# Dilated attention's third head group: 64x64 class blocks in place of masked 128x128 tiles

## The chip, the core and the metric

One core of a Trainium2 chip runs the whole program, one transformer sub-layer for 1024 tokens in float32. The metric is the device time of one execution in microseconds. The program uses TensorE (PE, with its weight loads shown apart as PEld), VectorE (DVE), ScalarE (ACT), GpSimd (POOL), and SyncE (SP), which issues nearly all DMAs.

## The reference, cut to what matters

The block has three mixers beside each other. The change touches the first, a sliding-window attention in three head groups, of window and dilation (128, 1), (512, 4), (2048, 16), with eight heads of 64 each:

```python
def dilated_window_attention(q, k, v, window, dilation):
    half = window // (2 * dilation)                  # 64 in each group
    L = s // dilation                                # 1024, 256, 64
    # regroup positions into residue classes mod dilation, each of L positions
    ...
    valid = (|qpos - kpos| <= half) & (0 <= kpos < L)
    sc = where(valid, q @ k * dh ** -0.5, -1e30)
    m = max(sc); p = exp(sc - m); l = sum(p)
    return (p / l) @ v, m + log(l)

outs, lses = one of these per group
wts = softmax(stack(lses), axis=0)
oa = einsum('gbsh,gbshd->bshd', wts, stack(outs))
```

In the third group the dilation is 16, so there are 16 classes of 64 positions, and with a half window of 64 each position of a class sees all 64 positions of its own class and nothing else. A tile of 128 queries, ordered by class, holds two classes: of its 128 x 128 scores with the same 128 keys, only the two diagonal blocks of 64 x 64 count.

## The kernel before

The program is one long run of PE work in stages: norms and key/value projections, the axial attention, value and key projections of the dilated attention, the dilated attention itself, then the merge gates, the three output branches and the last projection. The dilated attention takes the stretch from 716 to 987 us.

Its work is cut into twelve *items*, one for each pair of heads `p_` (four) and group `g` (three), in the order of `seq` (L1721), the third group of a pair last. While an item runs, PE also computes the dense query projection of an item two further on (`dense`, L139: 48 matmuls of 128 x 128 by 128 x 512 in each of two halves, float32r). `weave` (L176) lays the two streams into one order: it gives every piece of an item a cost, and between two pieces it issues as many dense matmuls as that cost is of the item's total. The order of ACT, DVE, POOL and SP in this stretch is the order in which the program writes the instructions; nothing reorders them.

An item works on eight tiles `T` of 128 queries, for both heads of its pair. `plan` (L1571) lists its pieces:

- `values(x)` (L1408): DMAs on SP that bring one half of V from DRAM to `vfull` (shown as `avs`), and for groups one and two also to `vpart` (`avp`). For the third group there are two per half, L1414, one for each class of a tile, with 64 partitions and pieces of 128 floats (both heads).
- `scores(b)` (L1449): for four tiles, the query tile of each head (64 rows of the array, the head's own half) times the keys, into PSUM banks of pool `s1` (four). Two tiles share a pair of banks. The two heads of a tile write different banks. L1466 in the profile.
- `soft(T)` (L1469): for each head a DVE instruction that adds the mask and takes the minimum of a row (L1478; the queries carry a minus sign), then an exponential with its row sum on ACT (L1479). Results lie in `pra`, five buffers.
- `trans(T)` (L1482): the probabilities are transposed on PE, one 128 x 128 transpose for each head and block of keys (L1505 where a tile has no 64-key blocks, L1496 otherwise), into a bank of pool `t` (two), and ACT copies them to `app` (L1508), six buffers. It comes `LAG` = 3 tiles behind `soft`: `trans(T - 3)` is written ahead of `soft(T)`, the last three in the next item.
- `pv(b)` (L1511): for four tiles, V of a head (64 weight columns, so the head's own column half of the array) times the transposed probabilities, all into one bank of pool `t` (L1522); ACT copies it out (L1530). `pv(0)` comes at `T` = 7, `pv(1)` at `T` = 3 of the next item, each followed by the `scores` of a half.
- `stats` (L1532): minima and sums are transposed and sent to DRAM; with them `combine` (L1634) weighs the three groups of a pair, in pieces that fall into the next pair's first two items.

`window` (L40) gives the keys of a tile and where its mask lies. In the third group a tile has one block of keys, its own 128; the mask at columns 256 to 383 lets a query see its own class only. The sums then hold exact zeros for the other class.

Of the kernel before, what the change touches and what calls it, by code (L numbers as in the profile page):

```python
# [8 lines left out]
F32 = mybir.dt.float32  # L9
# [8 lines left out]
P = 128  # L18
# [20 lines left out]

def window(g, T):  # L40
    if g == 2:
        return T * 128, T * 128 + 128, 256
    L = S // DIL[g]
    c0 = (T * 128) // L * L
    lo = max(T * 128 - 64, c0)
    hi = min(T * 128 + 192, c0 + L)
    return lo, hi, lo - (T * 128 - 64)
# [3 lines left out]
def block(ctx: ExitStack, tc: tile.TileContext, x, xT, memT, cst, msk, bcst, tabA, gpost,  # L51
# [1251 lines left out]
    with tc.tile_pool(name="aa", bufs=1, reuse_waits="tile") as aa:  # L1303
# [95 lines left out]
        def item(p_, g):  # L1399
# [8 lines left out]
            def values(x):  # L1408

                v = vdr[g, p_]  # L1410
                if g == 2:
                    vv = v.rearrange("(u r) f -> u r f", r=16)
                    for z in range(2):
                        nc.sync.dma_start(vfull[z * 64:z * 64 + 64, 4 * x:4 * x + 4].rearrange("p b h d -> p b (h d)"),  # L1414
                                          vv[:, 8 * x + z:8 * x + 8:2])
                    return
                if g == 0:
                    b0, b1 = (0, 4) if x == 0 else (4, 7)
                    nc.sync.dma_start(vfull[:, b0:b1].rearrange("p b h d -> p b (h d)"),
                                      v[64 + 128 * b0:64 + 128 * b1].rearrange("(b q) f -> q b f", q=128))  # L1420
                else:
                    nc.sync.dma_start(vfull[:, 4 * x:4 * x + 2].rearrange("p b h d -> p b (h d)"),
                                      v.rearrange("(u r) f -> u r f", r=4)[64:192, 2 * x:2 * x + 2])
                for z in range(2):
                    zs, f = slice(z * 64, z * 64 + 64), slice(z * 64, z * 64 + 64)
                    if g == 0:
                        nc.sync.dma_start(vpart[zs, 4 * x, z], v[960 * x:960 * x + 64, f])
                    else:
                        for e in range(2):
                            nc.sync.dma_start(vpart[zs, 4 * x + e:4 * x + 4:2, z], v[768 * e:768 * e + 256].rearrange(  # L1430
                                "(q r) f -> q r f", r=4)[:, 2 * x:2 * x + 2, f])
# [17 lines left out]
            def scores(b):  # L1449
                if b == 0:  # L1450
                    d["ops"] = OPS.pop((p_, g))
                    d["sts"] = cb.tile([P, 2, 2, NT], F32, name="sts", bufs=2)
                qa, ka = d["ops"]["q"], d["ops"]["k"]
                for j in range(4):
                    T = 4 * b + j
                    lo, hi, _ = window(g, T)
                    n = hi - lo
                    if j % 2 == 0:
                        banks = [pss1(), pss1()]
                    raws[T] = [x[:, j % 2 * 256:j % 2 * 256 + n] for x in banks]  # L1460
                    for r in range(2):
                        for h in range(2):
                            if r < len(spans(T, h)):
                                k0, k1, c = spans(T, h)[r]
                                hs = slice(h * 64, h * 64 + 64)
                                PE.matmul(raws[T][h][:, c:c + k1 - k0], qa[hs, T * 128:T * 128 + 128], ka[hs, k0:k1],  # L1466
                                          start=True, stop=True)
# [14 lines left out]
            def trans(T):  # L1482
                lo, hi, mo = window(g, T)
                n = hi - lo
                pr = st[T]
                kb = blocks_of(T)
                tp = pst()
# [23 lines left out]
            def pv(b):  # L1511
                if b == 0:
                    d["og"] = OG[p_, g] = cb.tile([P, S], F32, name="og", bufs=4)
                og = d["og"]
                ov = pst().rearrange("p a b -> p (a b)")
                for j in range(4):
                    terms = st.pop(4 * b + j)
                    n = len(terms[0])
                    for i in range(n):
                        for h in range(2):  # L1520
                            (vt, x), z, pp = terms[h][i]
                            PE.matmul(ov[h * 64:h * 64 + 64, j * 128:j * 128 + 128], vt[:, x, z], pp,  # L1522
                                      start=i == 0, stop=i == n - 1)
                if g == 0:
                    dst, src = og[:, b * 512:b * 512 + 512], ov
                else:
                    r = DIL[g] // 2
                    dst = og.rearrange("p (u r) -> p r u", r=DIL[g])[:, b * r:b * r + r]
                    src = ov.rearrange("p (r u) -> p r u", r=r)
                A.activation(dst, src, AF.Copy)  # L1530
# [694 lines left out]
def layout(inp):  # L2225
# [42 lines left out]
    k = np.arange(256)[None]  # L2268
    m = np.zeros((P, 768), f)
    m[:, :256] = np.where(np.abs(p + 64 - k) <= 64, 0.0, 1e30)  # L2270
    m[:, 256:384] = np.where(p // 64 == k[:, :128] // 64, 0.0, 1e30)
    m[:, 384:576] = np.concatenate([m[:, 128:256], m[:, 64:128]], 1)
    m[:, 576:768] = np.concatenate([m[:, 128:192], m[:, 0:128]], 1)
    r['msk'] = m
# [55 lines left out]
```

## Time and profile before

| | |
|---|---|
| median of three runs | 1414.94 us (1414.56 to 1415.76) |
| profiled execution, from its first to its last instruction | 1412.1 us |
| dilated attention, 716 to 987 us | 271 us, PE busy 269.2 |
| scores of a half, third group (L1466, in the chain) | 1.09 us |
| product with V of a half, third group (L1522, in the chain) | 1.02 us |
| a pair of transposes between dense matmuls (L1505) | 0.22 us |

In the profile's rows, a group of instructions has its line, engine, operation, tiles written and read, shape (for PE the rows and columns of the array that are used, then the partitions and elements moved), count, busy time in us and mean ns of one. "<-" behind an idle time names what ended it. A busy PE is no proof of a full one, since matmuls overlap; the distance between starts tells more. Times in the rows of the timeline and the chain are us from the span's start, then the length.

### The profile page before, as it was taken

Reading aid. Unit: us, or ns where it says so; the run is one execution under the profiler, and the core shown is the slowest. Engines: PE = TensorE matmul, PEld = TensorE weight load, DVE = VectorE, ACT = ScalarE, POOL = GpSimd, SP = SyncE. Lnnn points to the kernel's source line nnn. Section 1 sums busy time; section 2 is a strip of 40 time slices with the busy share of each in tenths; the row PEclk is TensorE's granted clock in tenths of the full one; section 3 lists DMA queues with packets and bytes.
Section 4 is the critical chain, followed back from the end, with each engine's and each line's share of the span. In section 5 each row is a group of like instructions: output and inputs, shape, how many; then the busy total and the mean of one; then the engine's idle time right before and its main releaser. Section 6 shows DMA issues by size and latency. Waiting matters only on the chain.

```text
span 1412.1 us, 21576 instructions
## 1 busy us (share of the span) xinstructions
PE 1389.9 (98%) x7640; PEld 1126.2 (80%) x7640; DVE 1054.0 (75%) x1839; ACT 665.0 (47%) x1414; POOL 500.3 (35%) x390
## 2 busy tenths in 40 slices
PE   7999999999999999999999999999999999999997
PEld 7799986666666889888888878787888888888886
DVE  7768677767763688788875777765878788677977
ACT  6544365666555445222146666656443334222332
POOL 0416702666657000333153353520423331035303
PEclk9999999999999999999999999999999999999999
DMA  6356532322210787445643554555343543866255
GB/s 235 101 179 211 186 109 86 116 83 71 83 55 25 243 261 240 125 148 175 201 140 90 135 162 115 138 144 180 106 150 127 176 175 124 323 216 207 94 206 179
DMA packets 121852, 216.01 MB, mean 153 GB/s; under 512 B 25424, under 2 KB 58000, under 8 KB 121744
## 3 DMA queue, kind: packets, MB, share of 16 engines
q1 hardware_dynamic: 106096, 189.17, 42.0%
q10 hardware_dynamic: 15648, 25.47, 4.9%
q8 instruction: 60, 0.98, 0.3%
q14 instruction: 48, 0.39, 0.1%
HBM read 149.21 MB, written 65.37 MB: 152 GB/s over the span
## 4 chain that ended last, share of the span: by engine, by line
PE 88%; DVE 4%; ACT 3%; DMA 2%; POOL 2%; issue 1%; SPq 0%; DVEq 0%; ACTq 0%; POOLq 0%
PE s L125 23%; PE sc L125 9%; PE d L143 7%; PE d L147 6%; PE d L145 6%; PE s L1177 4%; PE s L2101 4%; PE ov L809 4%; PE s L1226 3%; PE tr L1522 3%; PE s L1466 3%; PE s L794 2%; PE s L793 2%; PE tr L775 2%; PE d L2101 2%; PE d L550 1%
## 5 line engine op out<-in xcount | busy, mean ns | idle before, releaser
L143 PE MATMUL d<-hh,wh 128*128 128x512 f32 x480 | 195.1, 406 | 2.4 <-DVE fth L228 2.4
L145 PE MATMUL d<-hl,wh 128*128 128x512 f32 x480 | 194.3, 405 | 0.0
L147 PE MATMUL d<-hh,wl 128*128 128x512 f32 x480 | 190.9, 398 | 0.0
L800 POOL TENSOR_TENSOR bl<-bl,bp 128x512 f32<-128x512 f32 x96 | 130.6, 1361 | 54.4 <-ACT bp L796 49.0
L105 ACT ACTIVATE wh<-wr 128x512 fp32r<-128x512 f32 (+1 forms) x93 | 72.5, 787 | 122.1 <-PE sc L125 75.3
L106 DVE TENSOR_TENSOR wl<-wr,wh 128x1024 fp32r<-128x1024 f32 (+1 forms) x67 | 85.3, 1285 | 50.2 <-ACT wh L105 50.2
L125 PE MATMUL sc<-hh,wh 128*128 128x512 f32 x384 | 118.5, 389 | 0.0
L143 PEld LDWEIGHTS d<-hh,wh 128*128 128x128 f32 x480 | 90.5, 188 | 27.8 <-issue 6.6
L147 PEld LDWEIGHTS d<-hh,wl 128*128 128x128 f32 x480 | 90.6, 189 | 21.0 <-issue 4.5
L1479 ACT ACTIVATE pra<-pra,sts 128x192 f32<-128x192 f32 (+2 forms) x192 | 84.3, 442 | 46.3 <-DVE sts L1478 45.8
L145 PEld LDWEIGHTS d<-hl,wh 128*128 128x128 f32 x480 | 90.6, 189 | 19.2 <-issue 4.5
L796 ACT ACTIVATE bp<-s 128x512 f32<-128x512 f32 x128 | 75.7, 595 | 43.3 <-PE s L794 42.3
L776 DVE TENSOR_REDUCE bn<-tr 128x1 f32<-128x512 f32 x128 | 84.9, 683 | 12.8 <-PE tr L775 11.7
L125 PEld LDWEIGHTS sc<-hh,wh 128*128 128x128 f32 x384 | 72.1, 188 | 14.9
L1330 DVE SCALAR_TENSOR_TENSOR t2a<-d,tab 32x512 f32<-32x512 f32 x96 | 65.9, 687 | 23.2 <-PE d L147 21.4
L2006 POOL TENSOR_TENSOR acc<-acc,th 128x1024 f32<-128x1024 f32 x15 | 41.4, 2757 | 109.1 <-DVE th L2005 109.1
L1789 POOL TENSOR_TENSOR sf<-wr 128x512 f32<-128x512 f32 x22 | 29.8, 1373 | 131.3 <-DVE ch L106 57.4
L125 PE MATMUL sc<-hl,wh 128*128 128x512 f32 x192 | 74.8, 389 | 0.0
L125 PE MATMUL s<-hh,ch 128*128 128x512 f32 x224 | 73.5, 390 | 0.0
L1334 POOL TENSOR_TENSOR aq<-t1a,t2a 128x512 f32<-128x512 f32 x24 | 44.6, 1861 | 72.0 <-DVE t1a L1333 72.0
L1819 ACT ACTIVATE rs<-rs,hbm 128x512 f32<-128x512 f32 x44 | 31.8, 722 | 76.5 <-DVE rs L1818 75.8
L1397 POOL TENSOR_TENSOR ak<-kraw,kswp 128x512 f32<-128x512 f32 x24 | 47.8, 2015 | 54.7 <-DMA std<-sr 21.2
(500 smaller groups left out, 3775.6 us busy)
## 6 DMA issues: line engine op xcount, KB each, us to landing
wr<-in_wu SPq DMA_DIRECT2D x64, 512.0 KB
th<-thd SPq DMA_DIRECT2D x24, 512.0 KB
thd<-rs ACTq DMA_DIRECT2D x44, 256.0 KB
kd<-vy ACTq DMA_DIRECT2D x32, 256.0 KB
g2d<-fth SPq DMA_DIRECT2D x24, 256.0 KB
wos<-os SPq DMA_DIRECT2D x12, 512.0 KB
kraw<-kd SPq DMA_DIRECT2D x12, 512.0 KB
kswp<-kd SPq DMA_DIRECT2D x48, 128.0 KB
```

The source lines that it names most:

```text
L105: A.activation(dst_h, src, AF.Copy)
L106: V.tensor_tensor(dst_l, src, dst_h.bitcast(F32), op=OP.subtract)
L125: PE.matmul(out_ps, a, b, start=i == 0, stop=i == n - 1)
L143: PE.matmul(dst, wh[:, k, :], hh[k][:, t], start=k == 0, stop=False)
L145: PE.matmul(dst, wh[:, k, :], hl[k][:, t], start=False, stop=False)
L147: PE.matmul(dst, wl[:, k, :], hh[k][:, t], start=False, stop=k == 7)
L776: fp["last"] = V.tensor_reduce(st[i]["n"][:, j, c:c + 1], s, axis=AX.X, op=OP.min)
L796: A.activation(pp, s, AF.Exp, scale=-1.0)
L800: G.tensor_tensor(lsum[i % 2], lsum[i % 2], pp, op=OP.add)
L1330: V.scalar_tensor_tensor(t2[i], p[j], -0.125, tab[1][j, t], op0=OP.mult, op1=OP.mult)
L1479: A.activation(src, src, AF.Exp, scale=-1.0, bias=bias, accum_out=sts[:, h, 1, T:T + 1])
L2101: PE.matmul(dst[:, e[0]:e[1]], a, b, start=k == 0 and q == 0, stop=k == 3 and q == 2)
```

## The change

For the third group (`g == 2`), and for nothing else:

- `scores`: each head's 128 x 128 product becomes two of 64 x 64, one for each class `z`. Query class `z` is the weight (64 rows, 64 columns) and writes the partitions `z` of the head's bank, 64 columns wide. Four matmuls for a tile in place of two.
- `window` gives 64 columns instead of 128, so `soft` works on 64 columns for a head, and the two heads lie beside each other in 128 columns of `pra`. The mask is not changed at the place where it is now read (columns 256 to 319, which are zero there since the line that wrote the class mask is gone).
- `trans`: one transpose of these 128 columns turns both heads of a tile at once. It is written only for odd `T`, for the tile and its even neighbour together, with one copy on ACT for both.
- `pv`: the transposed tile has head `h`'s keys on the partitions of that head, so V of head `h` and class `z` must lie on those partitions too. Four matmuls of 64 x 64 by 64 columns for a tile in place of two of 128 x 64 by 128.
- `values`: the DMAs bring one head each (64 partitions, 8 classes, pieces of 64 floats) in place of one class each.

```diff
 def window(g, T):
     if g == 2:
-        return T * 128, T * 128 + 128, 256
+        return T * 128, T * 128 + 64, 256
...
                 if g == 2:
                     vv = v.rearrange("(u r) f -> u r f", r=16)
-                    for z in range(2):
-                        nc.sync.dma_start(vfull[z * 64:z * 64 + 64, 4 * x:4 * x + 4].rearrange("p b h d -> p b (h d)"),
-                                          vv[:, 8 * x + z:8 * x + 8:2])
+                    for h in range(2):
+                        hs = slice(h * 64, h * 64 + 64)
+                        nc.sync.dma_start(vfull[hs, 4 * x:4 * x + 4].rearrange("p b z d -> p (b z) d"),
+                                          vv[:, 8 * x:8 * x + 8, hs])
                     return
...
                     raws[T] = [x[:, j % 2 * 256:j % 2 * 256 + n] for x in banks]
+                    if g == 2:
+                        for z in range(2):
+                            for h in range(2):
+                                hs, zs = [slice(i * 64, i * 64 + 64) for i in (h, z)]
+                                t = slice(T * 128 + z * 64, T * 128 + z * 64 + 64)
+                                PE.matmul(raws[T][h][zs], qa[hs, t], ka[hs, t], start=True, stop=True)
+                        continue
...
             def trans(T):
                 lo, hi, mo = window(g, T)
                 n = hi - lo
+                if g == 2:
+                    if T % 2:
+                        tp = pst()
+                        pp = aa.tile([P, 4, 128], F32, name="app", bufs=6)
+                        for z in range(2):
+                            PE.transpose(tp[:, z, :], st[T - 1 + z][:, 0:128], ident)
+                            st[T - 1 + z] = pp[:, z]
+                        A.activation(pp[:, :2], tp[:, :2], AF.Copy)
+                    return
...
                     terms = st.pop(4 * b + j)
+                    if g == 2:
+                        for z in range(2):
+                            for h in range(2):
+                                hs, zs = [slice(i * 64, i * 64 + 64) for i in (h, z)]
+                                PE.matmul(ov[hs, j * 128 + z * 64:j * 128 + z * 64 + 64], vfull[hs, 4 * b + j, z], terms[hs, zs],
+                                          start=True, stop=True)
+                        continue
...
     m[:, :256] = np.where(np.abs(p + 64 - k) <= 64, 0.0, 1e30)
-    m[:, 256:384] = np.where(p // 64 == k[:, :128] // 64, 0.0, 1e30)
```

## The prediction, made before the change was run

> **What bounds the kernel now.** I read the page's busy shares and chain first, then the sums of the stretch in which the dilated attention runs, then the chain through one of its third-group items.
>
> ```profile
> span 1412.1 us, 21576 instructions
> PE 1389.9 (98%) x7640; PEld 1126.2 (80%) x7640; DVE 1054.0 (75%) x1839; ACT 665.0 (47%) x1414; POOL 500.3 (35%) x390
> PE 88%; DVE 4%; ACT 3%; DMA 2%; POOL 2%; issue 1%; SPq 0%; DVEq 0%; ACTq 0%; POOLq 0%
> ...
> 716.00:987.00 271.00, 269.23 (x2068) 219.09 (x2066) 188.00 (x572) 174.92 (x560) 101.51 (x51) 1.00 0.49 136
> ```
>
> The last row has the columns PE, PEld, DVE, ACT, POOL busy, granted clock, DMA share, GB/s. PE idles 1.8 of 271 us there, at full clock, while DVE has 83 us free and ACT 96. A microsecond taken from PE's own stream is therefore nearly a microsecond off the end, and work taken from DVE or ACT counts only where PE waits for it. The chain through the first third-group item (start, length, what):
>
> ```profile
> 765.23 1.90 PE tr L1522 x32
> 767.12 1.09 PE s L1466 x16
> 768.22 0.37 PE tr L1505 x2
> ...
> 771.36 0.22 PE tr L1505 x2
> ...
> 774.59 1.02 PE tr L1522 x16
> 775.61 1.94 PE s L1466 x17
> ```
>
> L1466 is the scores of four tiles (half an item), L1505 the two transposes of a tile, L1522 the product with V for four tiles. Eight f32 matmuls show as 16 records, so a matmul is two passes. How passes share the array is read from the busy sums of one line over growing windows (length, PE busy, instructions begun):
>
> ```profile
> 774.52:774.67 0.15, 0.15 (x2) 1.00 0.00 0
> 774.52:774.78 0.26, 0.26 (x4) 1.00 0.00 0
> 774.52:774.89 0.37, 0.37 (x6) 1.00 0.00 0
> 774.52:775.34 0.82, 0.82 (x16) 1.00 0.00 0
> ...
> 767.05:767.26 0.21, 0.20 (x2) 1.00 0.00 0
> 767.05:767.37 0.32, 0.32 (x4) 1.00 0.04 6
> 767.05:767.48 0.43, 0.42 (x6) 1.00 0.03 5
> ```
>
> The first four are V's product, the rest the scores. Passes come in pairs, one pair per 0.11 us: both heads work at once, in two column halves of the array for V's product and in two row halves for the scores. So a half costs eight pair steps, 8 x 0.11 = 0.88 us, plus about 0.2 us to the next kind of work in the chain rows above (1.09 and 1.02).
>
> **The change, part by part.**
>
> *Transposes.* Per item eight pairs become four. A pair between dense matmuls costs PE 0.22 us (771.36). Four items: 16 x 0.22 = 3.5 us less. Nothing hides them now; they stand on the chain.
>
> *Scores.* Per tile two matmuls of 64 rows, 128 weight columns and 128 moved columns become four of 64, 64 and 64. Rows for the size of a pass (mean ns of one):
>
> ```profile
> L1466 PE MATMUL s<-ak,aq 64*128 64x128 f32 x208 | 25.0, 285 | 0.0
> L1466 PE MATMUL s<-ak,aq 64*128 64x64 f32 x80 | 13.2, 245 | 0.0
> L1466 PEld LDWEIGHTS s<-ak,aq 64*128 64x128 f32 x464 | 33.8, 187 | 5.1 <-issue 4.5
> L1522 PEld LDWEIGHTS tr<-app,avs 128*64 128x64 f32 x480 | 26.7, 137 | 9.5 <-ACT pra L1479 3.6 <-ACT wh L105 2.9 <-ACT app L1508 2.3
> ```
>
> 64 moved columns fewer shorten a matmul by 40 ns, 64 weight columns fewer shorten a load by 50 ns; both are about half of the 0.11 us step, so I take a 64 by 64 pass at 0.058 us. There are 32 passes in a half. If all four blocks of a tile (two heads, two classes) run together, that is eight steps: 8 x 0.058 = 0.46 us against 0.90, 0.44 less. If the two classes of a head take turns, it is 16 steps: 0.93, 0.03 more. A third bound is the rate at which PE takes instructions: a half will have 64 (loads and passes) instead of 32.
>
> ```profile
> 774.51 0.20 PEld L1522 LDWEIGHTS tr<-app,avs 128*64 128x64 f32 x4 [0.37 <-ACT wh L105]
> 774.52 0.33 PE L1522 MATMUL tr<-app,avs 128*64 128x128 f32 x2
> ```
>
> Four loads of 0.137 us lie within 0.20 us and two passes begin with them: six instructions in 0.06 us, 10 ns each, and so 64 in 0.64 us. I take 0.55, between 0.46 and 0.64: 0.35 less a half, 2.8 us in eight halves; bounds 3.5 less and 0.2 more.
>
> The Trainium skill states a floor that speaks against this: "TensorE: Matmul & The Clock Gate", Part 1, "Wait — 56ns, not 53.3ns?", has starts of matmuls never closer than about 25 ns, however small. By it a score half would be an estimated 32 x 25 = 0.80 us, and my sum would end at 1411.1. The two passes that begin together in the last row above speak against it for passes in different parts of the array.
>
> *Product with V.* Per tile two matmuls (128 rows, 64 weight columns, 128 moved) become four of 64, 64, 64, in diagonal quarters of the array: the heads can run side by side as now, the two classes of a head follow each other. 16 steps of 0.058 = 0.93 us for 0.87: 0.06 more a half, 0.45 us in all. Bounds: nothing more (16 x 0.055), or 0.87 more a half, 7.0 in all, if a step stays at the 0.109 us below which no f32 pair of passes lies in these windows. I take the low side because of the halved load and matmul rows.
>
> *DVE, ACT.* The masked minimum and the exponential of a tile and head shrink from 128 to 64 columns, and 16 of the 32 copies of 256 columns go:
>
> ```profile
> L1478 DVE CUSTOM_DVE_ANT_0 pra<-s,mask 128x192 f32<-128x192 f32 x80 | 24.8, 353 | 2.3 <-PE s L1466 1.8
> L1478 DVE CUSTOM_DVE_ANT_0 pra<-s,mask 128x128 f32<-128x128 f32 x64 | 15.7, 286 | 4.7 <-PE s L1466 4.5
> L1479 ACT ACTIVATE pra<-pra,sts 128x192 f32<-128x192 f32 x80 | 35.5, 446 | 25.7 <-DVE sts L1478 25.5
> L1479 ACT ACTIVATE pra<-pra,sts 128x128 f32<-128x128 f32 x64 | 25.0, 392 | 19.0 <-DVE sts L1478 19.0
> L1508 ACT ACTIVATE app<-tr 128x256 f32<-128x256 f32 x32 | 12.2, 381 | 6.6 <-PE tr L1505 6.4
> ```
>
> By the steps between sizes that is 67 ns of DVE and 54 of ACT for each of 64, 4.3 and 3.5 us, and 16 x 0.38 = 6.1 us of ACT. All of it lies beside PE and is worth nothing except at PE's idle times:
>
> ```profile
> 823.70 0.33 PE L1496 MATMUL tr<-cs,pra 128*128 128x128 f32 x1 [0.25 <-ACT app L1508]
> ...
> 885.98 0.33 PE L1496 MATMUL tr<-cs,pra 128*128 128x128 f32 x1 [0.22 <-ACT app L1508]
> ...
> 941.83 0.44 PE L1522 MATMUL tr<-app,avs 128*64 128x128 f32 x4 [0.80 <-ACT app L1508]
> ...
> 983.75 0.33 PE L1505 MATMUL tr<-cs,pra 128*128 128x128 f32 x1 [0.43 <-ACT og L1530]
> ...
> 818.03 2.53 DVE L1677 TENSOR_TENSOR og<-og,wgt 128x1024 f32<-128x1024 f32 x1
> 820.59 1.38 DVE L1330 SCALAR_TENSOR_TENSOR t2a<-d,tab 32x512 f32<-32x512 f32 x2
> 822.00 0.29 DVE L1478 CUSTOM_DVE_ANT_0 pra<-s,mask 128x128 f32<-128x128 f32 x1
> 822.39 0.40 ACT L1479 ACTIVATE pra<-pra,sts 128x128 f32<-128x128 f32 x1 [1.63 <-DVE sts L1478]
> 823.18 0.47 ACT L1508 ACTIVATE app<-tr 128x384 f32<-128x384 f32 x1
> ```
>
> At 823.70 and 885.98, just behind the first score half of an item, PE waits for a copy that ACT makes behind the item's first two exponentials, which wait for DVE, full since 818.03. That gate opens 0.067 + 2 x 0.054 = 0.17 us sooner, while PE comes 0.35 sooner: 0.17 of the scores' gain is lost at each, 0.35 us together. The 0.80 us at 941.83 lie in the second group's item and stay. At 983.75 PE waits with the last item's seventh pair of transposes, which no longer exists; the pair that comes later finds the copy done: 0.35 of the 0.43 us go (bounds 0 and 0.43).
>
> *Moved steps and waits.* An even tile's transpose is issued with its odd neighbour's, where that one's already stands, so the last pair ahead of V's product (771.36) keeps its place 3.2 us ahead of it, and its copy of 0.38 us its cover. The even tile's buffer lives one step longer: four of five are then in use. No new wait; PSUM banks for transposes are asked for half as often.
>
> *Loads of V.* Two DMAs a half as before, in pieces of 256 instead of 512 bytes. Queue rows of a stretch of 3.0 us with nearly only 512-byte packets, one of 2.7 us with 256-byte ones, and SP's issue:
>
> ```profile
> q1 hardware_dynamic: 544, 0.26, 30.5%
> ...
> q1 hardware_dynamic: 474, 0.11, 18.4%
> ...
> 769.29 1.28 SPq L1414 DMA_DIRECT2D avs<-vdr  x2
> ```
>
> A packet takes 0.305 x 16 x 3.0 / 544 = 27 ns, or 0.184 x 16 x 2.7 / 474 = 17 ns. A half load goes from 512 x 27 / 16 = 0.86 us of the engines to 1024 x 17 / 16 = 1.09. It is issued at 769.29 for a product near 784, a cover of over 10 us; what is behind it on SP (weights, raw keys) is used a unit later. Nothing, or 0.2 us at each of eight loads if that cover were gone.
>
> **Sum.** -3.5 (transposes) -2.8 (scores) +0.45 (V) +0.35 (gates) -0.35 (end) = -5.85 us on a span of 1412.1. The median of the runs, 1414.94, is 2.8 above that span, which I carry over: 1409.1 us.
>
> **Rivals.** *The two classes of a head take turns in the scores.* For it: no row shows all four quarters at work. Against it: the windows show column halves together and row halves together. Scores +0.2, V +0.45, no gate loss but the two gates 0.17 sooner (-0.35), end -0.35, transposes -3.5: -3.55, 1411.4 us. Chance 0.20.
>
> *The two heads take turns in the product with V.* They now use different row halves but still write one bank; the scores, which do use row halves, write two banks, so no row tests it. Then a half is 32 steps, 1.86 us, 0.93 more than in my sum, 7.4 in eight: +1.6, 1416.5 us, slower than before. It decides from four fifths of the passes on (5.85 of 7.4). Against it: V's product shows pairs in one bank today, though over all rows. The Trainium skill ("TensorEngine Tiling (Array Packing)", "Gotcha 1: PSUM Pressure") states that row tiles cannot access one bank at the same time; it has no word on row tiles that also differ in columns, and no row here shows it. Chance 0.12.
>
> *PE is fed too slowly.* In the 0.82 us window V's product takes 16 passes and as many loads, 26 ns each; were that its limit, a half of 64 would last 1.66 us, scores and V together 12.4 us more, and with -3.5 and -0.7 the end is +8.2, 1423.1 us. It decides from 18 ns on. Against it: the 10 ns above. Chance 0.09.
>
> *DVE and ACT gate more.* If half of the gain goes into waits of PE: 1412.0 us. For it: DVE full behind the score halves of two items; against: 83 us free. Chance 0.09.
>
> **How the numbers follow.** The forecast has 0.50, with its own range from 1407.0 (score half 0.46, V unchanged, all of the four idle times gone but the second group's) to 1410.8 (score half 0.75, idle times nearly as now). From 1407.0 to 1413.0 lie nearly all of it, the first rival and the last: 0.78. A measurement of this kernel tells about 0.2%, 2.8 us, from no change: faster (below 1412.1) is the forecast, the first rival and half of the last, 0.73; within, the rest of it and most of the heads' taking turns, 0.15; slower 0.12.
>
> **What will show it.** Score half in the chain: 32 passes in about 0.75 us instead of 16 in 1.09; windows with four passes per 0.058 us (right), two (classes take turns). V's half: 32 passes in about 1.08; near 2 us means heads taking turns. Of L1505's 160 transposes 64 go and 32 come at a new line. DVE's smallest form near 0.22 us. PE's idle times of 716 to 987 stay at 1.5 to 2.2 us; over 4 would mean that DVE and ACT gate. If both halves grow in step with their instruction count, the feed was the limit. A stage that ends 6 us sooner but an end that does not follow would refute that PE's stream sets the end.

## The result and the profile after

| | before | after |
|---|---|---|
| median of five runs each | 1414.94 us (1413.20 to 1415.76) | 1409.91 us (1409.67 to 1411.43) |
| ratio, 95% interval | | 0.9962 [0.9949, 0.9974] |
| profiled execution, span | 1412.1 | 1408.1 |
| first third-group scores to first matmul of the gates ("the stage" below) | 230.34 | 225.03 |
| PE idle from 716 to 987 us | 1.77 | 2.86 |

The change is 5.0 us faster by the medians; 1409.1 us was predicted. The page of the changed kernel, in the same order as before (span, busy times, shares of the chain):

```profile
span 1408.1 us, 22008 instructions
PE 1384.0 (98%) x7864; PEld 1120.3 (80%) x7864; DVE 1051.2 (75%) x1839; ACT 655.7 (47%) x1398; POOL 501.9 (36%) x390
PE 86%; DVE 4%; ACT 4%; DMA 2%; POOL 2%; issue 2%; SPq 1%; DVEq 0%; ACTq 0%; POOLq 0%
```

The attention stretch in the sums of windows:

```profile
716.00:987.00 271.00, 268.14 (x2315) 218.90 (x2314) 188.43 (x575) 169.33 (x551) 106.25 (x54) 1.00 0.50 137
```

PE still bounds, at full clock, but its idle time in the stretch has grown from 271 - 269.23 = 1.77 to 2.86 us. To see what the stage itself won, take the distance between two rows of the chain: the start of the first third-group score half and of the first gate matmul (L125). Before:

```profile
756.82 1.09 PE s L1466 x16
...
987.16 12.96 PE s L125 x56
```

After, with the rows of an item between them:

```profile
757.20 0.62 PE s L1467 x32
...
766.79 0.62 PE s L1467 x32
...
770.32 0.23 PE tr L1498 x2
...
783.73 1.08 PE tr L1539 x32
...
982.23 17.91 PE s L125 x78
```

987.16 - 756.82 = 230.34 against 982.23 - 757.20 = 225.03: 5.31 us less in the stage. The span shows only 4.0, since the start lies 0.38 later and the tail behind 982.23 is 0.93 longer (425.87 for 424.94), in a part that the change does not touch; two later runs (the pair without key adds, below) have equal tails of 425.30, so that is not counted against the change. The median is 2.8 us above the span before (1414.94 - 1412.1) and 1.8 after; in every run of the kernel of before beside the experiments below a run's time is 1.7 to 1.8 above its own span. So the profiled execution of before was about 1 us quicker than the median, which fits the span's 4.0 beside the median's 5.0.

The score half went from 1.09 to 0.62 us, the product with V from 1.02 to 1.08. The sums of windows that grow from the start of one score half show why (length, PE busy, matmuls begun, clock):

```profile
766.72:766.76 0.04, 0.04 (x4) 1.00 0.07 10
766.72:766.82 0.10, 0.10 (x4) 1.00 0.04 4
766.72:766.88 0.16, 0.16 (x8) 1.00 0.40 105
...
766.72:766.99 0.27, 0.27 (x16) 1.00 0.24 62
```

Four passes begin together and four more every 0.055 to 0.06 us: all four quarters of the array work at once. The same for the product with V:

```profile
783.66:783.70 0.04, 0.04 (x2) 1.00 0.15 13
...
783.66:783.82 0.16, 0.16 (x4) 1.00 0.04 3
783.66:783.88 0.22, 0.22 (x6) 1.00 0.03 2
```

Two passes per 0.06 us: the heads run side by side in one bank, the two classes of a head in turn. The groups by line and shape:

```profile
L1486 DVE CUSTOM_DVE_ANT_0 pra<-s,mask 128x64 f32<-128x64 f32 x64 | 11.4, 219 | 3.8 <-PE s L1467 3.6
...
L1498 PE MATMUL tr<-cs,pra 128*128 128x128 f32 x32 | 6.3, 277 | 0.0
...
L1467 PE MATMUL s<-ak,aq 64*64 64x64 f32 x256 | 6.1, 225 | 0.1
```

32 transposes are left at the new line and the minimum fell from 286 to 219 ns, as said. What did not come out as said are the waits. PE's timeline:

```profile
823.64 0.33 PE L1513 MATMUL tr<-cs,pra 128*128 128x128 f32 x1 [0.95 <-ACT app L1525]
...
884.58 0.44 PE L1513 MATMUL tr<-cs,pra 128*128 128x128 f32 x2 [0.76 <-ACT app L1525]
```

These were 0.25 and 0.22. The waits of PE's weight loads, summed by what released them (sum, times, longest):

```profile
PEld s L1474 <- DVE sts L1486: 1.1, 3, 0.5
```

This one is new: at three *joints*, where an item's product with V is followed by the next item's first scores, these wait for banks that DVE frees with the third group's last minima. They do not show as idle time of PE, but in the distances between starts: from the first of these score matmuls to the next dense one it is 2.47, 2.13 and 2.31 us, and was 1.94 before. The third-group score half at 817.43 is late in the same way, 1.20 us to the next dense matmul instead of 0.62. The wait at 983.75 is gone. What DVE and POOL do ahead of 823.64, after:

```profile
815.09 0.69 DVE L106 TENSOR_TENSOR wl<-wr,wh 128x512 fp32r<-128x512 f32 x1 [1.40 <-ACT wh L105]
815.99 1.65 DVE L106 TENSOR_TENSOR wl<-wr,wh 128x512 fp32r<-128x512 f32 x1 [0.20 <-ACT wh L105]
...
818.11 2.56 DVE L1701 TENSOR_TENSOR og<-og,wgt 128x1024 f32<-128x1024 f32 x1
...
815.82 2.95 POOL L1397 TENSOR_TENSOR ak<-kraw,kswp 128x512 f32<-128x512 f32 x2 [4.93 <-DMA std<-sr]
...
824.99 1.29 POOL L1334 TENSOR_TENSOR aq<-t1a,t2a 128x512 f32<-128x512 f32 x1 [0.83 <-DVE t1a L1333]
```

and before:

```profile
816.87 0.69 DVE L106 TENSOR_TENSOR wl<-wr,wh 128x512 fp32r<-128x512 f32 x1 [0.20 <-ACT wh L105]
...
817.15 4.57 POOL L1397 TENSOR_TENSOR ak<-kraw,kswp 128x512 f32<-128x512 f32 x2 [5.37 <-DMA std<-sr]
```

L106 on DVE splits a weight tile for the dense projection, L1397 on POOL adds the two parts of the rotated keys. Before, DVE began first, its split took 0.69 us and POOL's two adds, which met the weighing at 818.03 as well, took 4.57. After, POOL began 0.17 us ahead, its two adds took 2.95 and DVE's split 1.65. The end of the split at 817.64 is what the last minima, the weighing at 818.11 and the third group's first minima queue behind. PE's stream had come 0.9 us sooner by then (a dense matmul at 787.90 of before begins at 787.03), while the weighing begins 0.08 later. Ahead of each of the three joints a pair of splits meets two of POOL's adds too: the pairs took 3.21, 2.87 and 3.05 us after (at 772.17, 834.21 and 895.15), 2.57, 2.51 and 2.53 before, and the joint behind the longest pair waits longest (0.52, 0.19 and 0.36).

The other place is different. DVE and POOL ahead of 884.58, after:

```profile
877.69 0.69 DVE L106 TENSOR_TENSOR wl<-wr,wh 128x512 fp32r<-128x512 f32 x1 [0.20 <-ACT wh L105]
...
878.85 2.76 DVE L1701 TENSOR_TENSOR og<-og,wgt 128x1024 f32<-128x1024 f32 x1
...
878.45 4.31 POOL L1397 TENSOR_TENSOR ak<-kraw,kswp 128x512 f32<-128x512 f32 x2 [5.85 <-DMA std<-sr]
```

Here the split is done before POOL begins and takes its 0.69 us. What lies beside the adds is the weighing: 2.76 us, where it took 2.53 before (at 880.31) and takes 2.0 in the runs without these adds, below. PE's score half is 0.47 shorter, the weighing 0.23 longer, and the way from its end to the start of ACT's copy 0.17 shorter (2.62 us before, 2.45 after): 0.47 + 0.23 - 0.17 = 0.53, and the wait grew by 0.54.

The Trainium skill ("SBUF — State Buffer", "Who interferes with whom") states that a DVE instruction with two SBUF inputs contends with a GpSimd instruction that reads SBUF, and it calls the ports that the two engines share an exclusive lock: the one that issues first has them for the whole instruction and the other is blocked (said there of DVE's two-port modes). The rows of this instruction agree with that to within 0.2 us: a split of 0.69 that starts beside an add of 1.29 us (the last row of POOL after, an add of the same shape by itself) would end at 815.82 + 1.29 + 0.69 = 817.80 if it stood through the whole add, and ended at 817.64. The weighing of 2.0 us, standing through the first add at the other place, would end at 878.45 + 1.29 + 2.0 = 881.74, and ended at 881.61.

### The profile page after: what moved, and what is told of

Read it like the earlier page. It is cut to its first block, busy times and chain, and to the rows that moved or that the text cites. A ratio compares the mean times of both kernels' runs of the same rounds, so it can differ in the third digit from the quotient of the medians.

```text
span 1408.1 us, 22008 instructions
## 1 busy us (share of the span) xinstructions
PE 1384.0 (98%) x7864; PEld 1120.3 (80%) x7864; DVE 1051.2 (75%) x1839; ACT 655.7 (47%) x1398; POOL 501.9 (36%) x390
## 3 DMA queue, kind: packets, MB, share of 16 engines
q8 instruction: 62, 1.02, 0.3%
## 4 chain that ended last, share of the span: by engine, by line
PE 86%; DVE 4%; ACT 4%; DMA 2%; POOL 2%; issue 2%; SPq 1%; DVEq 0%; ACTq 0%; POOLq 0%
PE s L125 24%; PE sc L125 9%; PE d L143 6%; PE d L147 6%; PE d L145 6%; PE s L1177 4%; PE s L2125 4%; PE ov L809 3%; PE s L1226 3%; PE s L794 2%; PE s L793 2%; PE tr L775 2%; PE d L2125 2%; PE s L1474 2%; PE tr L1546 1%
## 5 line engine op out<-in xcount | busy, mean ns | idle before, releaser
L106 DVE TENSOR_TENSOR wl<-wr,wh 128x1024 fp32r<-128x1024 f32 (+1 forms) x67 | 85.6, 1289 | 52.1 <-ACT wh L105 52.0
L125 PE MATMUL sc<-hh,wh 128*128 128x512 f32 x384 | 118.7, 390 | 0.0
L1487 ACT ACTIVATE pra<-pra,sts 128x192 f32<-128x192 f32 (+2 forms) x192 | 80.9, 423 | 54.3 <-DVE sts L1486 54.1
L125 PEld LDWEIGHTS sc<-hh,wh 128*128 128x128 f32 x384 | 72.0, 188 | 15.7 <-DVE wh L106 0.4
L125 PE MATMUL sc<-hl,wh 128*128 128x512 f32 x192 | 74.7, 389 | 0.0
L125 PE MATMUL s<-hh,ch 128*128 128x512 f32 x224 | 73.7, 390 | 0.0
L1397 POOL TENSOR_TENSOR ak<-kraw,kswp 128x512 f32<-128x512 f32 x24 | 45.9, 1939 | 51.7 <-DMA std<-sr 20.0
```

The costliest lines, as they stand in the source:

```text
L106: V.tensor_tensor(dst_l, src, dst_h.bitcast(F32), op=OP.subtract)
L125: PE.matmul(out_ps, a, b, start=i == 0, stop=i == n - 1)
L1487: A.activation(src, src, AF.Exp, scale=-1.0, bias=bias, accum_out=sts[:, h, 1, T:T + 1])
```

## The experiments

All stage lengths are read from the chain as above, PE idle time and the splits' mean from the windows and groups of 716 to 987 us. Ratios are to the kernel of before, run beside each set; its median was 1415.90 us beside e1, e2, e4 and e5, 1415.22 beside e3, e10, e8 and b8, and 1415.05 beside the rest, so runs of different sets are better compared by ratio than by median. The changed kernel was not run again in these sets. A difference from it carries two intervals, together about 2 us, and where it is smaller the reading rests on the traces, one execution each.

| run | median us | ratio, 95% interval | stage us | PE idle us | split L106, mean ns |
|---|---|---|---|---|---|
| before | 1414.94 | | 230.34 | 1.77 | 877 |
| after | 1409.91 | 0.9962 [0.9949, 0.9974] | 225.03 | 2.86 | 964 |
| e1_scores_only | 1412.52 | 0.9979 [0.9970, 0.9988] | 228.26 | 3.03 | 933 |
| e2_full_scores | 1413.33 | 0.9983 [0.9974, 0.9992] | 229.50 | 3.36 | 1005 |
| e4_weigh_earlier | 1411.94 | 0.9973 [0.9962, 0.9985] | 227.95 | 4.53 | 969 |
| e5_joints_later | 1411.87 | 0.9979 [0.9970, 0.9988] | 229.50 | 6.07 | 1033 |
| e3_own_transposes | 1411.82 | 0.9976 [0.9966, 0.9986] | 226.33 | 3.67 | 948 |
| e10_twice_transposed | 1410.85 | 0.9974 [0.9965, 0.9983] | 226.27 | 2.03 | 883 |
| e8_weigh_on_pool | 1413.44 | 0.9985 [0.9976, 0.9994] | 229.96 | 5.72 | 1147 |
| b8_before_weigh_on_pool | 1417.63 | 1.0019 [1.0010, 1.0028] | 234.00 | 3.74 | 1017 |
| e11_no_key_add | 1406.71 | 0.9941 [0.9927, 0.9954] | 222.01 | 1.18 | 777 |
| b11_before_no_key_add | 1413.73 | 0.9990 [0.9981, 0.9999] | 229.29 | 1.22 | 760 |
| e12_key_add_t7 | 1416.46 | 1.0013 [1.0004, 1.0022] | 231.37 | 6.54 | 1378 |
| e13_key_add_t6 | 1417.68 | 1.0021 [1.0012, 1.0030] | 231.87 | 7.22 | 1350 |

### The parts of the change

**The scores alone.** The kernel of before with the 64 x 64 score blocks and 64-column minima; transposes and product with V keep their number and shape.

```diff
+                    if g == 2:
+                        for z in range(2):
+                            for h in range(2):
...
+                                PE.matmul(raws[T][h][zs], qa[hs, t], ka[hs, t], start=True, stop=True)
+                        continue
...
-                            PE.transpose(tp[:, k, :], pr[:, h * n + c:h * n + c + 128], ident)
+                            PE.transpose(tp[:, k, :], pr[:, h * n * (g < 2) + c:h * n * (g < 2) + c + 128], ident)
```

> The kernel before with only the scores in 64x64 blocks and the softmax on 64 columns; two transposes a tile and V's product of 128 columns stay as before (they read the same 128 columns twice, so the third group's result is left out). Theory (PE's stream sets the end, but DVE and ACT hold PE at the places behind the first score half of an item): PE's score halves shrink by 0.47 us each, 3.8 us in eight, but 1.5 to 2 us come back as waits of PE, so 2 us less than before. Rival (all of PE's saving reaches the end): 3.8 us less.

Measured: 0.9979, 3.0 us faster by the ratio, and 2.08 less in the stage. Each score half is 0.62 us in the chain, 0.47 less, which makes 3.8 in eight; the waits rose at the same places as in the changed kernel, in PE's timeline to 0.96 at the first:

```profile
824.72 0.55 PE L1503 MATMUL tr<-cs,pra 128*128 128x128 f32 x3 [0.96 <-ACT app L1515]
```

So about 1.7 of the 3.8 us that PE saves on scores are waited away in this execution, as the theory said. The time does not decide: its interval, 1.7 to 4.2 us, holds the theory's 2 and the rival's 3.8.

**All but the scores.** The changed kernel with scores of 128 x 128 again.

```diff
-                        for z in range(2):
-                            for h in range(2):
-                                hs, zs = [slice(i * 64, i * 64 + 64) for i in (h, z)]
-                                t = slice(T * 128 + z * 64, T * 128 + z * 64 + 64)
-                                PE.matmul(raws[T][h][zs], qa[hs, t], ka[hs, t], start=True, stop=True)
+                        for h in range(2):
+                            hs = slice(h * 64, h * 64 + 64)
+                            t = slice(T * 128, T * 128 + 128)
+                            PE.matmul(banks[h][:, j % 2 * 256:j % 2 * 256 + 128], qa[hs, t], ka[hs, t], start=True, stop=True)
```

> The changed kernel with the scores multiplied as before, 128x128 for each head; the softmax still reads 64 columns of them, so the choice of the class is left out. Theory: the waits of PE that the changed kernel has go back with the score halves' length, so the narrow scores are worth only 1.5 to 2 us at the end and this kernel takes 1.5 to 2 us more than the changed one. Rival (PE's saving reaches the end in full): 3.8 us more than the changed one.

Measured: 0.9983, 2.4 us faster than before, and so 3.0 us slower than the changed kernel by the ratios and 4.47 in the stage. The theory's 1.5 to 2 us misses; the rival's 3.8 is nearer. By times the two parts add up: 0.9979 x 0.9983 = 0.9962, the ratio of the whole change. By the stage they don't: 2.08 and 0.84 make 2.9 of 5.31, since this execution too met DVE late (0.30 and 0.91 us ahead of the score halves at 819.38 and 882.67, 0.67 each at 825.03 and 888.31; splits of 1005 ns). One execution places the parts only to about 1 us.

**Each tile transposed by itself.** The even tile's transpose goes back to its own step, with its own bank and copy.

```diff
-                    if T % 2:
-                        tp = pst()
...
-                        for z in range(2):
-                            PE.transpose(tp[:, z, :], st[T - 1 + z][:, 0:128], ident)
-                            st[T - 1 + z] = pp[:, z]
-                        A.activation(pp[:, :2], tp[:, :2], AF.Copy)
+                    tp = pst()
...
+                    PE.transpose(tp[:, 0, :], st[T][:, 0:128], ident)
+                    A.activation(pp[:, 0], tp[:, 0], AF.Copy)
+                    st[T] = pp[:, 0]
```

> The changed kernel, but each third-group tile is transposed in its own step and copied by itself (32 copies of 128 columns instead of 16 of 256, 32 PSUM buffers asked for instead of 16); the number of transposes, 32, is unchanged. Theory (the gain of the transposes is their number, 0.11 us of PE each; the copies lie beside PE): within 0.8 us of the changed kernel, about 1410 us, and PE's idle times grow by less than 1 us. Rival (the gain comes from having one place and one buffer for two tiles: a fixed cost per place of about 0.1 us, or waits for buffers and copies): 1.6 us or more slower than the changed kernel, about 1411.5 to 1413 us, with new PE waits on ACT's copies at the single transposes.

Measured: 0.9976, 1.9 us above the changed kernel, though the two intervals overlap; 1.30 more in the stage, PE idle 0.81 more. By the median the theory misses (0.8) and the rival's number (1.6 or more) holds; by the idle time the theory holds, and the rival's waits on the single copies do not show: apart from the one shown next, the waits that grew are for DVE's minima (0.56 at 899.78) and in the second group's item (1.31 at 941.06, 0.95 in the changed kernel). One wait is told apart cleanly, that of the last item's seventh tile:

```profile
981.39 0.33 PE L1496 MATMUL tr<-cs,pra 128*128 128x128 f32 x1 [0.43 <-ACT og L1552]
```

It is the row at 983.75 of before, back with its 0.43 us as soon as that tile has a step of its own. So pairing was worth this wait, and the rest of the difference is not settled.

**Every tile transposed twice**, so that there are 64 transposes again.

```diff
                         for z in range(2):
+                            PE.transpose(tp[:, 2 + z, :], st[T - 1 + z][:, 0:128], ident)
                             PE.transpose(tp[:, z, :], st[T - 1 + z][:, 0:128], ident)
```

> The changed kernel with every third-group tile transposed a second time into unused columns of the same PSUM buffer, so 64 transposes again as before the change, with nothing else touched. Theory (a pair of transposes costs the end 0.22 us, and 16 pairs are back): 3.5 us slower than the changed kernel, about 1413.4 us, or 0.4 less where the waits on DVE behind the first score halves (0.95 and 0.76 us) swallow two of the pairs. Rival (the transposes fill time in which PE would wait anyway, since DVE gates the stage after the change): 1.7 us or less slower, below 1411.7 us.

The chain shows each place 0.22 us longer, four transposes of 0.11 where there were two:

```profile
770.83 0.11 PE tr L1498
770.94 0.11 PE tr L1499
771.05 0.11 PE tr L1498
771.16 0.11 PE tr L1499
```

and PE's timeline shows the second of the two waits shrunk:

```profile
884.94 0.44 PE L1514 MATMUL tr<-cs,pra 128*128 128x128 f32 x2 [0.27 <-ACT app L1526]
```

Yet the stage grew by 1.24 us, not 3.5, and the time by 0.9 (medians) to 1.7 (ratios). The rival's number holds. PE's idle time fell by 0.83 us (the wait at 884.94 from 0.76 to 0.27), and the 1.1 us of waits of the joints' scores for DVE are gone from the sums of waits. At the changed kernel's working point, then, more than half of a microsecond taken from PE came back as a wait in this execution. The splits' mean fell as well, from 964 to 883 ns: the pairs of splits ahead of the three joints, which meet POOL's adds, took 2.43 to 2.47 us (772.90, 834.83, 895.97) in place of 2.87 to 3.21. So part of the return is a collision that fell out shorter, and the run does not tell how large a part. The cost of a pair was right; that nothing hides it holds for the kernel before and not for the one after.

### Where the waits come from

**The weighing two tiles sooner.** `STEP_T` places the weighing's steps by tile.

```diff
-        STEP_T = (7, 7, 7, 3, 3, 7, 2)
+        STEP_T = (7, 7, 7, 3, 3, 5, 2)
```

> The changed kernel with the third weighing of a finished head pair (2.5 us of DVE) two tiles earlier in the second group's item, away from the joint with the third group's first scores. Theory (DVE, full with that weighing, holds the minima and so ACT's copies and PE): PE's waits of 0.95 and 0.76 us near 823.6 and 884.6 and the late score half at 818 go, 1.5 to 2.2 us less than the changed kernel. Rival (the waits come from ACT's own queue or from the PSUM banks of the transposes): no difference, within 0.3 us.

Measured: the waits at 823 and 884 are gone, so DVE set them and not ACT or PSUM. But PE waits ahead of the scores instead, for DVE:

```profile
818.89 0.73 PE L1467 MATMUL s<-ak,aq 64*64 64x64 f32 x16 [1.64 <-DVE sts L1486]
...
881.26 0.73 PE L1467 MATMUL s<-ak,aq 64*64 64x64 f32 x16 [1.94 <-DVE sts L1486]
```

and the kernel is no faster than the changed one, where the theory had 1.5 to 2.2 us.

**The joints later**, more dense matmuls between the product with V and what follows.

```diff
-SOFT, JOINED, LAG = 1000.0, 300.0, 3
+SOFT, JOINED, LAG = 1000.0, 1000.0, 3
```

> The changed kernel with the cost of a joint (V's product and the next half's scores) raised from 300 to 1000, so some three more dense matmuls stand between the last softmax of an item and the joint. Theory (the next item's first scores wait for PSUM banks that DVE frees with the item's last minima): the 0.24 to 0.58 us lost at these three joints go, about 1 us less than the changed kernel. Rival (they wait for the loads of V in smaller pieces): no difference at these places, as the loads are issued at the same point of SP's order.

Measured: the joints' waits vanish, and larger ones stand elsewhere, 2.12 us at 824.15 the longest, PE idle 6.07 us in all. Again no faster.

**The weighing's multiply on POOL**, after and before.

```diff
-                V.tensor_tensor(ogv, ogv, wv, op=OP.mult)
+                (G if g == 2 else V).tensor_tensor(ogv, ogv, wv, op=OP.mult)
```

> The changed kernel with the third group's weighing multiply (2.6 to 2.8 us of DVE at 818.11 and 878.85, two tiles ahead of the first minima of a third-group item) done by POOL. Theory (DVE's lateness behind the weighing causes the PE waits of 0.95 and 0.76 us at 823.64 and 884.58 and part of those at the joints): both waits below 0.2 us, 1.0 to 2.5 us faster than the changed kernel, 1407.5 to 1409 us. Rival (POOL becomes the gate: its multiply of about 2.4 us comes ahead of the rotated queries and keys that it adds): new PE waits on POOL at the next items' first scores of 1 us or more, no faster than the changed kernel, 1410 to 1413 us.

> The kernel of before with the third group's weighing multiply done by POOL, beside the run of the changed kernel with the same edit. Theory (before, DVE's lateness cost PE only 0.25 and 0.22 us at the two places): 0.3 to 0.8 us faster than before, 1414.1 to 1414.6 us on the scale of the runs shown, and the change is worth 6 to 7 us between this pair instead of 5. Rival (POOL is the gate, or the change's lost gain has another cause): no faster than before, and the pair differs by 5 us or less.

Measured: the two waits are gone in the changed kernel, and it is slower all the same, by 3.3 us in the ratios; the kernel of before loses 2.7, and the pair differs by 4.2 us, not the 6 to 7 of the theory. The timelines of POOL, DVE and PE at the dearest place, in the run of the changed kernel:

```profile
933.52 2.95 POOL L1701 TENSOR_TENSOR og<-og,wgt 128x1024 f32<-128x1024 f32 x1
936.55 2.69 POOL L1703 TENSOR_TENSOR og<-og 128x1024 f32<-128x1024 f32 x1
...
935.38 4.41 DVE L106 TENSOR_TENSOR wl<-wr,wh 128x512 fp32r<-128x512 f32 x2 [1.73 <-ACT wh L105]
...
941.57 0.48 PE L1546 MATMUL tr<-app,avs 128*64 128x128 f32 x2 [3.92 <-ACT app L1525]
```

Two splits that take 0.69 each alone end 4.41 us after they began, at 939.79, beside two long instructions of POOL that end at 939.24; six minima queue behind them and PE waits 3.92 us (3.41 at the same place in the kernel of before with this edit, where 0.80 stands without it). The rival's "no faster" holds, but no wait of PE on POOL shows, and neither theory nor rival had this place. It named the mechanism for the next pair.

**No key adds beside the splits.** In both kernels the keys are loaded as they are, without POOL's adds.

```diff
         def k_add(p_, g):
-            kr, ks = KK.pop((p_, g))
             ka = OPS.setdefault((p_, g), {})["k"] = ab.tile([P, S], F32, name="ak", bufs=2)
-            for x in range(2):
-                t = half[x]
-                G.tensor_tensor(half_of(ka, x, g), classes(kr[:, t], g), classes(ks[:, t], g), op=OP.add)
+            nc.sync.dma_start(ka, kd[0, p_ * 3 + g])
```

> The changed kernel with POOL's rotation adds of the keys left out in the attention stage (ak is loaded raw by one DMA; the swapped keys are not loaded; the scores are therefore those of unrotated keys). Theory (part of the change's gain is eaten by DVE coming late to the last minima and to the weighing, because its 0.69 us weight splits last 1.5 to 4.4 us beside POOL's adds): the splits' mean falls from 0.96 to below 0.85 us, the PE waits at 823.6 and 884.6 fall below 0.4 us, the stage ends 2 us or more sooner, and the change is worth 6 to 7.5 us between this pair of kernels instead of 5. Rival (DVE has too much work of its own there, as after the weighing was moved): the two waits stay above 0.6 us and the pair differs by 5 us or less.

> The kernel of before with the same adds left out. Theory: PE's waits in the attention stage were only 1.8 us, so 0 to 1 us faster than before (ratio 0.9993 to 1.0000), and the changed kernel without the adds is 6 to 7.5 us faster than this one (ratio to before 0.994 to 0.995). Rival: the pair differs by 5 us or less.

Measured: the pair differs by 7.0 us in the medians and 7.28 in the stage, as the theory said, where 5.0 and 5.31 stand with the adds. The groups of the changed kernel without them, by line and shape:

```profile
L106 DVE TENSOR_TENSOR wl<-wr,wh 128x512 fp32r<-128x512 f32 x27 | 20.6, 777 | 25.7 <-ACT wh L105 25.7
```

and its timeline of DVE and PE:

```profile
814.52 0.69 DVE L106 TENSOR_TENSOR wl<-wr,wh 128x512 fp32r<-128x512 f32 x1 [0.20 <-ACT wh L105]
...
820.69 0.44 PE L1505 MATMUL tr<-cs,pra 128*128 128x128 f32 x2 [0.16 <-ACT app L1517]
...
880.88 0.44 PE L1505 MATMUL tr<-cs,pra 128*128 128x128 f32 x2 [0.17 <-ACT app L1517]
```

The split that took 1.65 us takes 0.69, the two waits are 0.16 and 0.17, and the joints wait no more. In the kernel of before without the adds PE has no wait at these two places. DVE's own instructions are unchanged, so this refutes that its load alone gates PE. The difference of the differences, 2 us, is within the intervals of the times and rests on the traces, in which the named waits are gone. The edit also takes the loading of the swapped keys and some 47 us of POOL's work out of the stretch; that it is the collisions, and not these, is argued from the instructions that got shorter (the split 0.69 for 1.65, the weighing 2.03 and 2.02 for 2.56 and 2.76) and from the next two runs, which keep both. By this reading the collisions eat 2 us of the change's gain. The kernel of before gains only 1.05 us of stage by the same edit.

**The key adds one and two tiles later**, a try at a version that beats both.

```diff
-                if it and it["ahead"] and T in (1, 5):
+                if it and it["ahead"] and T in (1, 7):
```

> The changed kernel with the key adds of POOL asked for two tiles later (at tile 7 of an item instead of tile 5), behind the weighing's sum instead of beside the weight split ahead of the last minima. Theory (the collision of the adds with the split at 815.99 and 878 is what makes the weighing late): the waits at 823.6 and 884.6 fall below 0.5 us; 0.5 to 2 us faster than the changed kernel unless the adds meet other splits, 1408 to 1409.5 us. Rival (the collision only moves to the splits some us later): new PE waits of about the same sum, 1409.5 to 1411.5 us.

> As the run before, with the key adds one tile later (tile 6). Theory: the adds then start beside the last minima and the weighing, not beside the split; the waits at 823.6 and 884.6 fall by 0.3 to 0.8 us, 1408.5 to 1409.7 us. Rival: no change beyond 0.5 us, or slower by new waits, 1409.7 to 1411.5 us.

(The second has 6 in place of 7.) Measured: both are slower than before, outside what theory and rival said. DVE, POOL and PE at one of the new waits, in the timeline of the first:

```profile
856.39 4.00 DVE L106 TENSOR_TENSOR wl<-wr,wh 128x512 fp32r<-128x512 f32 x2 [2.56 <-ACT wh L105]
...
855.37 4.47 POOL L1397 TENSOR_TENSOR ak<-kraw,kswp 128x512 f32<-128x512 f32 x2
...
860.72 0.48 PE L1474 MATMUL s<-ak,aq 64*128 64x128 f32 x2 [0.42 <-DVE sts L1486]
```

and its splits in the groups:

```profile
L106 DVE TENSOR_TENSOR wl<-wr,wh 128x512 fp32r<-128x512 f32 x26 | 35.0, 1378 | 24.2 <-ACT wh L105 24.2
```

The adds now meet the pair of splits in eight of twelve cases: 1378 ns in the mean instead of 964, and 6.54 us of PE idle. At the two places that the edit was made for, the first run did what its theory said: the splits there took 0.69 us, the weighing met no add and took 2.03 and 2.04, and the waits fell to 0.41 (at 825.01) and 0.43 (at 888.13). They are not gone, so the collisions are not all that makes DVE late there. In the second run the weighing met the adds (2.57 and 2.55 us) and the waits stayed at 0.87 and 0.96. The theory that later is better falls; that collisions cause waits is borne out from the other side. Over the runs of the table PE's idle time goes with the splits' mean, 1.2 us at 760 to 777 ns, 2.9 at 964, 6.5 to 7.2 at 1350 to 1378, but for the two runs in which the order itself was pulled apart (the weighing sooner, the joints later). No version with the whole computation beat the changed kernel.

## Why the prediction was right, step by step

- **Transposes, -3.5: right at the place, too simple at the end.** A pair between dense matmuls costs 0.22 to 0.23 us in the chain after, 16 are gone, and the doubled run puts 0.22 back at each. But the doubled run ends only 1.24 us later in the stage, as the saved time is partly waited away.
- **Scores, -2.8: mis-sized.** 0.47 less a half and 3.8 in eight, a little beyond the bound of 3.5, which had 0.90 - 0.46 = 0.44 a half. All four quarters work at once, so the turn-taking rival falls. The term was too small because I took 0.55, half way to a feed of 10 ns an instruction: by the windows 16 passes and their loads begin in 0.27 us, about 8 ns each. The rival of a slow feed (18 ns and more) falls with it, as does the floor of 25 ns between starts that the prediction took from the Trainium skill ("TensorE: Matmul & The Clock Gate", Part 1): four passes begin within 0.04 us.
- **Product with V, +0.45: right**, 1.08 for 1.02 in the chain, 0.5 in eight. Two passes per 0.06 us in one bank refute heads taking turns. The rule of the Trainium skill ("TensorEngine Tiling (Array Packing)", "Gotcha 1: PSUM Pressure") that row tiles cannot access one bank at the same time does not bite for two row halves that also differ in columns.
- **The gates, +0.35: the step that failed.** The reading was that the copies behind the first score halves come 0.17 us sooner by what DVE's and ACT's shorter instructions save, while PE comes 0.35 sooner, 0.17 of wait at each. The 0.17 is there (2.62 to 2.45 us behind the weighing). But the waits grew by 0.70 and 0.54, 1.24 in all, and 1.1 more stands at the joints, which no step had; PE idles 2.86 us where 1.5 to 2.2 were to show the forecast. What the step left out is that DVE's instructions last longer beside POOL's: ahead of the joints the pairs of splits took about 0.5 us more; at the first place the split took 1.65 us, so the weighing began no sooner while PE came 0.9 sooner; at the second the weighing itself took 0.23 longer, and PE's score half had gained 0.47, not 0.35. Without the adds the waits go from none before to 0.16 and 0.17 after, the growth that the step gave.
- **The end, -0.35: right.** The wait at 983.75 is gone, and comes back when the even tile has a step of its own (0.43).
- **The sum.** -5.85 was said, the stage shows -5.31: -3.5 - 3.8 + 0.5 + 1.24 + 1.1 - 0.43 = -4.9. Smaller things that the rows show beside it nearly cancel: the late score half at 817.43 (+0.58), the wait at 941.83, now 0.95 at 939.34 (+0.15), and three of the removed pairs of transposes that stood 0.44 us in the chain before and not 0.22 (825.44, 887.72 and 983.75: -0.66). About 0.4 us of the stage is not placed. The scores' 1.0 too little and the waits' 2 too little cancel by half, so the number was better than its parts, and that is luck. "DVE and ACT gate more" had 1412.0 for half of the gain lost; about a quarter was lost (2 of 7.3), so it was a share of the outcome, not the outcome.
- **Carrying the difference of span and median over was sound.** It sets the change against the median, not against a profiled execution that was about 1 us quicker than the median. The spans alone differ by 4.0 us, the medians by 5.0 and the stage by 5.3.

## What to carry to other kernels

When an engine is 98% busy, time taken from it is worth its full size only until the next engine's timing comes to the surface: look for the waits of 0.2 us as places where the gain will stop, and ask what the other engine is queued behind there. An instruction that shows two durations in one profile (a split of 0.69 and of 1.65 us) can be the sign of a collision, and who begins first can flip with a shift of less than a microsecond. Blocks that lie in different rows and columns of the array can be multiplied at the same time, so a block-diagonal product is worth cutting even into small matmuls.

## What was not expected of the hardware

In the dilated attention of these runs each of the four waits of PE of 1.94 us or more was followed by about half the granted clock for a while, which makes such a wait dearer than it looks; the waits of 1.64 us and less were not. In the run with the joints later, the wait of 2.12 us at 824.15 is followed by a granted clock of 0.50 (windows: length, PE, PEld, DVE, ACT, POOL busy, clock):

```profile
824.10:825.50 1.40, 1.35 (x5) 1.25 (x6) 1.36 (x6) 0.73 (x5) 0.00 (x0) 0.53 0.99 398
825.50:827.00 1.50, 1.50 (x5) 1.11 (x5) 1.31 (x10) 1.07 (x6) 0.65 (x1) 0.50 1.09 350
```

In the run with the weighing sooner, the wait of 1.94 us is followed by 0.55, but only 1.2 us later, and the one of 1.64 us by none (full clock throughout):

```profile
819.00:820.50 1.50, 1.50 (x22) 1.23 (x23) 1.46 (x4) 1.50 (x5) 1.50 (x2) 1.00 0.87 199
...
882.50:884.00 1.50, 1.50 (x7) 1.21 (x6) 1.44 (x6) 1.50 (x5) 0.80 (x1) 0.55 1.02 243
```

The Trainium skill ("TensorE: Matmul & The Clock Gate", "What's actually happening") has half clock after an idle window of about 3.4 us; here the clock fell behind waits of 1.94 and 2.12 us. Behind the longest two, 3.92 and 3.41 us (the weighing's multiply on POOL, after and before), it was 0.50 as well, for some 5 and 3 us.
